# Weight sums of the seven-product blocks: formed by accumulating transfers in layer 0 instead of on VectorE

## The chip, the cores and the metric

The kernel runs on one core of a Trainium2 chip. The metric is the device time of one execution in microseconds (us). Engines are named as in the profile: PE is TensorE (matrix products), PEld its weight load, DVE is VectorE, ACT is ScalarE, POOL is GpSimd, SP is SyncE. Transfers are issued by an engine's instruction stream: SP issues most loads, POOL a second stream of loads and stores. Rows "SPq" and "POOLq" tell the two apart.

## The reference

Two layers of a diffusion backbone over 512 latent tokens and 256 context tokens, model width 1024. Each layer is modulation, attention, then a SwiGLU feed-forward. Only the feed-forward of layer 0 is changed in how its work is done:

```
def swiglu(h, w_gate_up, w_down):
    g, u = jnp.split(h @ w_gate_up, 2, axis=-1)
    return (jax.nn.silu(g) * u) @ w_down

h_lat = h_lat + g_f * swiglu(modulate(h_lat, sh_f, sc_f), ffn_w_gate_up[l], ffn_w_down[l])
if ctx_out:            # layer 0 only
    h_ctx = h_ctx + cg_f * swiglu(modulate(h_ctx, csh_f, csc_f), ffn_w_gate_up[l], ffn_w_down[l])
```

The hidden width is 2816, that is 22 blocks of 128 columns, called j below.

## The kernel before

**Products in three parts.** Every fp32 operand is split into a high part (an ACT cast, L1401 or L308) and a low part (operand minus high part, DVE, L1402 or L309). One product is high·high, high·low and low·high, so three matmuls for each slice of 128 in the contraction (L1414, L1415, L1416).

**Seven products in place of eight.** In a feed-forward block j≥2 of layer 0, gate weights g and up weights u (each 128 x 1024) form a 2 x 2 block matrix with two halves of the contraction, g1, g2, u1, u2, each 128 x 512. The tokens form the other 2 x 2 matrix. Class Pair computes the four result blocks with seven block products: `head` does 11 (with g1) and 21 (with g2); `body` does T2 (with the weight sum s2), T3 (s3) and T1 (s1); `tail` does 22 (s4) and T4 (u2). One block product is 12 matmuls of 128 x 384. `sums()` forms the token sums once for each layer.

**Weights of one pair.** `weights()` loads g and u, 512 KB each, through SP into `wr` tiles, and forms on DVE s1 = u1+u2 (L1436, tile pl), s2 = s1−g1 (L1437, ph), s3 = g1−u1 (L1440, ph) and s4 = g2−s2 (L1444, pl). Then `parts` splits g, s2, s3, s1, s4 and u2 for PE. T3 and T2 share the `wh`/`wl` tile of s3 and s2; T1 and 22 share that of s1 and s4.

**Staging.** `ffn()` walks over chunks of hidden blocks: in layer 0 (0–3), (4–7), (8–11), (12–15), (16–19), (20–21). Blocks 0 and 1 do all eight products directly, so 20 pairs remain in layer 0, and 19 in layer 1. After a chunk, `down0` runs for 8 output blocks m: load home[m] through POOL (L1255, 384 KB), multiply the chunk with w_dn (L319–L322), add on DVE (L1251), store home[m] through POOL (L1568). The w_dn loads go through SP into `wr` tiles too.

**Other work laid beside it.** `late_mods` prepares modulation for layer 1 during this stage: a 512 KB load through POOL into one of the `rope` tiles (L263), then reductions on DVE (L273) that wait for its landing. Each step of it is placed by `late_step` at a point of the pairs.

**What sets the order.** A scheduler that simulates a timeline puts the instructions of every engine in order, and each engine then runs its own in that order. Tiles rotate: wr, wh and wl have 3 buffers each, ph and pl 4 each, p 8. A load into a tile waits until the last readers of that buffer are done.

Of the kernel before, what the change touches and what calls it, by code (L numbers as in the profile page):

```python
# [12 lines left out]
ALU = mybir.AluOpType  # L13

P = 128
# [71 lines left out]
def pieces(c):  # L87

    cut = [(slice(max(c.start, x.start), min(c.stop, x.stop)), v) for v, x in enumerate((LATS, CTXS))]
    return [(x, v) for x, v in cut if x.start < x.stop]  # L90
# [8 lines left out]
def hybrid_kernel(ctx: ExitStack, tc, I, out):  # L99
# [6 lines left out]
    def T(tag, shape, dt=F32):  # L106
        count[0] += 1
        if tag not in SIZES:
            return sb.tile(shape, dt, tag=tag, name=f"{tag}_{count[0]}", bufs=BUFS.get(tag, 1))
        n = int(np.prod(shape[1:]))  # L110
        t = sb.tile([P, SIZES[tag] // (2 if dt == mybir.dt.bfloat16 else 4)], dt, tag=tag, name=f"{tag}_{count[0]}",
                    bufs=BUFS[tag])[: shape[0], :n]
        if len(shape) == 3:
            t = t.rearrange("p (a b) -> p a b", a=shape[1])
        return t

    def B(dt=F32, tag="b"):
        return T(tag, [P, NT], dt)
# [12 lines left out]
    V, S, G, PE = nc.vector, nc.scalar, nc.gpsimd, nc.tensor  # L131

    def dma(o, i, eng=None):
        return (eng or nc.sync).dma_start(f(o), f(i))

    def f(ap):
        return ap.bitcast(F32) if ap.dtype == F32R else ap

    silu, marks = [], {}

    def behind(ins, *before):

        for x in before:
            tc.add_manual_dep(ins.ins, x.ins.name, mybir.DependencyInfo(mybir.DependencyClass.NoSync,
                              mybir.DependencyReason.DATA), reason="products in one run")
        return ins
# [148 lines left out]
    def mod(*which):  # L295
        while which not in MOD:
            bg()
        return MOD[which]
# [593 lines left out]
    for c in range(4):  # L892
# [9 lines left out]
        s0, m0, s1, m1 = turns_of  # L902
# [424 lines left out]
    def combined(src, l, comp, c1, c2):  # L1327

        ops = {x: [] for x in ("11", "12", "21", "22", "T1", "T2", "T3", "T4")}
        far, near, spare, w = [], [], [], c1.stop  # L1330
        at1, at2, at3 = (slice(i * w, i * w + w) for i in range(3))
        narrow, room = 3 * w <= NT, {}

        def unit(tag):

            if not room.get(tag):
                t = B(F32R, tag)
                room[tag] = [t[:, i * w : i * w + w] for i in range(NT // w)]
            return room[tag].pop(0)

        def modulated_to(t, src, k, r, c, at, after=()):
            for x, v in pieces(c):
                d = t[:, at + x.start - c.start : at + x.stop - c.start]
                behind(V.scalar_tensor_tensor(d, src[:, x], mod(l, comp + 1, v, k), r[:, x], op0=ALU.mult, op1=ALU.mult), *after)
                S.activation(d, d, AF.Identity, bias=mod(l, comp, v, k), scale=1.0)

        def several(t, names, tag):

            dst, n = (B(F32R, tag), B(F32R, tag)), len(names) * w
            h, lo = split(t[:, :n], dst=dst)  # L1350
            near_done.append(marks["split"])
            near_cast.append(marks["cast"])
            for i, x in enumerate(names):
                ops[x].append((h[:, i * w : i * w + w], lo[:, i * w : i * w + w]))
            return h[:, n:], lo[:, n:]

        def use(k, r, c, v):
            i, half = k % 4, k // 4
            at = w * half
            if c is c2:  # L1360
                if half == 0:
                    far.append(B())
                modulated_to(far[i], src[k], k, r, c, at)
                name, tag = ("12", "22")[half], ("st", "b")[half]
                if narrow and half == 0:
                    t = T(("ph", "pl")[i % 2], [P, 2 * w], F32R)
                    h, lo = t[:, :w], t[:, w:]
                else:
                    h, lo = unit(tag), unit(tag)
                ops[name].append(parts(far[i][:, at : at + w], h, lo))  # L1370
                return
            if half == 0:
                near.append(B(tag="p"))
            modulated_to(near[i], src[k], k, r, c, at, near_done[-2:-1])
            if half == 1:
                spare.append(several(near[i], ("11", "21"), "b"))

        def sums():

            for i in range(4):  # L1380
                tag = "st" if i < 2 else "b"
                x, y = B(tag="p"), B(tag="p")
                b11, b21, b12, b22 = near[i][:, at1], near[i][:, at2], far[i][:, at1], far[i][:, at2]
                V.tensor_tensor(x[:, at1], b12, b11, op=ALU.subtract)
                V.tensor_tensor(x[:, at2], b22, x[:, at1], op=ALU.subtract)
                if narrow:
                    V.tensor_tensor(x[:, at3], b22, b12, op=ALU.subtract)
                    several(x, ("T1", "T2", "T3"), tag)
                    V.tensor_tensor(y[:, at1], b21, x[:, at2], op=ALU.subtract)
                    ops["T4"].append(parts(y[:, at1], *spare[i]))  # L1390
                    continue
                several(x, ("T1", "T2"), tag)
                V.tensor_tensor(y[:, at1], b22, b12, op=ALU.subtract)
                V.tensor_tensor(y[:, at2], b21, x[:, at2], op=ALU.subtract)
                several(y, ("T3", "T4"), tag)

        near_done.clear(), near_cast.clear()
        return Norm(src, use, G if l else None, (0, 4, 1, 5, 2, 6, 3, 7)), ops, sums

    def parts(t, h, lo, after=()):  # L1400
        S.copy(h, t)  # L1401
        marks["low"] = behind(V.tensor_tensor(lo, t, f(h), op=ALU.subtract), *after)  # L1402
        return h, lo
# [14 lines left out]
    class Pair:  # L1418
# [7 lines left out]
        def weights(self):  # L1426
            h = [slice(0, 512), slice(512, 1024)]
            g, u = T("wr", [P, D]), T("wr", [P, D])
            dma(g, I["w_gu"][self.l, self.j, 0])
            dma(u, I["w_gu"][self.l, self.j, 1])  # L1430
            two = lambda: (T("wh", [P, D], F32R), T("wl", [P, D], F32R))
            w1, w2, w3 = two(), two(), two()
            parts(g, *w1, self.after)
            self.g1, self.g2 = ([x[:, y] for x in w1] for y in h)
            s1, s2 = T("pl", [P, 512]), T("ph", [P, 512])
            behind(V.tensor_tensor(s1, u[:, h[0]], u[:, h[1]], op=ALU.add), *self.after)  # L1436
            V.tensor_tensor(s2, s1, g[:, h[0]], op=ALU.subtract)  # L1437
            self.s2 = parts(s2, *(x[:, h[0]] for x in w2))
            s3 = T("ph", [P, 512])
            behind(V.tensor_tensor(s3, g[:, h[0]], u[:, h[0]], op=ALU.subtract), *self.after)  # L1440
            self.s3 = parts(s3, *(x[:, h[1]] for x in w2))
            self.s1 = parts(s1, *(x[:, h[0]] for x in w3))
            s4 = T("pl", [P, 512])
            V.tensor_tensor(s4, g[:, h[1]], s2, op=ALU.subtract)  # L1444
            self.s4 = parts(s4, *(x[:, h[1]] for x in w3))
            self.u2 = parts(u[:, h[1]], T("ph", [P, 512], F32R), T("pl", [P, 512], F32R))

# [10 lines left out]
        def body(self):  # L1458
            self.y = PG()[:, : self.w]
            product(self.z, self.s2, self.ops["T2"])  # L1460
            S.copy(self.t[:, self.c1], self.z)
            product(self.y, self.s3, self.ops["T3"], True)
            product(self.z, self.s1, self.ops["T1"])
            S.copy(self.t[:, self.c2], self.z)  # L1464
            self.done = marks["middle"] = V.tensor_tensor(self.t[:, self.c2], self.y, self.t[:, self.c2], op=ALU.add)

        def tail(self):
            product(self.z, self.s4, self.ops["22"])
            marks["silu"] = S.activation(self.s[:, self.c2], self.z, AF.Silu)
            product(self.y, self.u2, self.ops["T4"])  # L1470
            V.tensor_tensor(self.t[:, self.c1], self.y, self.t[:, self.c1], op=ALU.add)
            for c in (self.c2, self.c1) if self.w > NX else (slice(0, 2 * self.w),):
                V.tensor_tensor(self.s[:, c], self.s[:, c], self.t[:, c], op=ALU.mult)
                parts(self.s[:, c], *(x[:, c] for x in self.dst))
            self.done = marks["low"]
# [369 lines left out]
```

## Time and profile before

| what | value |
|---|---|
| median of 3 runs | 1554.84 us (1552.52 to 1556.6) |
| span of the profiled execution | 1553.0 us |
| PE busy | 1527.4 us, 98% of the span |
| DVE busy | 1179.9 us, 76% |
| ACT busy | 758.2 us, 49% |
| POOL busy | 195.1 us, 13% |
| feed-forward of layer 0 | about 455 to 955 us of the span |
| DMA queue of SP (q1) | 148.47 MB, 30.1% of 16 engines' span |
| DMA queue of POOL (q0) | 73.94 MB, 13.9% |

The profiled execution was not timed in another way than by its span, which lies 1.8 us below the median of the runs and within their spread. PE is nearly always busy, so what counts is the few places where PE stands still. The share of DVE says nothing by itself of the time.

### The profile page before, as it was taken

Reading aid. Unit: us, or ns where it says so; the run is one execution under the profiler, and the core shown is the slowest. Engines: PE = TensorE matmul, PEld = TensorE weight load, DVE = VectorE, ACT = ScalarE, POOL = GpSimd, SP = SyncE. Lnnn points to the kernel's source line nnn. Section 1 sums busy time; section 2 is a strip of 40 time slices with the busy share of each in tenths; the row PEclk is TensorE's granted clock in tenths of the full one; section 3 lists DMA queues with packets and bytes.
Section 4 is the critical chain, followed back from the end, with each engine's and each line's share of the span. In section 5 each row is a group of like instructions: output and inputs, shape, how many; then the busy total and the mean of one; then the engine's idle time right before and its main releaser. Section 6 shows DMA issues by size and latency. Waiting matters only on the chain.

```text
span 1553.0 us, 26645 instructions
## 1 busy us (share of the span) xinstructions
PE 1527.4 (98%) x10048; PEld 1375.5 (89%) x10048; DVE 1179.9 (76%) x2418; ACT 758.2 (49%) x1521; POOL 195.1 (13%) x266
## 2 busy tenths in 40 slices
PE   9999999999999999999999999999999999999997
PEld 8788887878999898999989998877789899899997
DVE  4799877776867686777768667789977779678685
ACT  4532676674555242432424335567856445354453
POOL 0022211000111102012021122560011000000001
PEclk9999999999999999999999999999999999999999
DMA  9775654244643636547475493210214223324322
GB/s 320 251 226 176 165 129 106 57 131 136 217 138 119 232 104 216 173 133 287 128 261 175 156 355 137 59 37 1 96 58 161 70 84 127 115 75 136 89 91 87
DMA packets 80930, 225.69 MB, mean 145 GB/s; under 512 B 11232, under 2 KB 18400, under 8 KB 80800
## 3 DMA queue, kind: packets, MB, share of 16 engines
q1 hardware_dynamic: 61968, 148.47, 30.1%
q0 software_dynamic: 17680, 73.94, 13.9%
q8 instruction: 79, 1.29, 0.3%
q10 hardware_dynamic: 1152, 1.57, 0.3%
q14 instruction: 51, 0.42, 0.1%
HBM read 186.97 MB, written 23.07 MB: 135 GB/s over the span
## 4 chain that ended last, share of the span: by engine, by line
PE 85%; DVE 7%; DMA 3%; ACT 2%; issue 2%; POOL 0%; SPq 0%; DVEq 0%; ACTq 0%; POOLq 0%
PE pso L530 5%; PE pss L1416 5%; PE pss L1415 5%; PE pss L1414 5%; PE psd L319 4%; PE pss L319 4%; PE psd L321 4%; PE psd L322 4%; PE pss L322 4%; PE pss L321 4%; PE pst L1416 3%; PE pst L319 3%; PE pst L321 3%; PE pst L1414 3%; PE pst L322 3%; PE pst L1415 3%
## 5 line engine op out<-in xcount | busy, mean ns | idle before, releaser
L308 ACT CAST wh<-wr 128x1024 fp32r<-128x1024 f32 (+2 forms) x148 | 115.6, 795 | 225.1 <-DMA wr<-in_w_dn_dram 39.4
L309 DVE TENSOR_TENSOR wl<-wr,wh 128x1024 fp32r<-128x1024 f32 (+2 forms) x145 | 131.1, 911 | 82.3 <-ACT wh L308 78.1
L537 ACT ACTIVATE p<-p,sm 128x512 f32<-128x512 f32 (+3 forms) x144 | 105.0, 730 | 30.6 <-DVE sm L541 30.1
L1414 PE MATMUL pss<-b,wh 128*128 128x384 f32 (+1 forms) x346 | 107.6, 312 | 0.5 <-ACT b L345 0.5
L1415 PE MATMUL pss<-b,wh 128*128 128x384 f32 (+1 forms) x346 | 107.8, 312 | 0.0
L1416 PE MATMUL pss<-b,wl 128*128 128x384 f32 (+1 forms) x346 | 107.1, 311 | 0.0
L321 PE MATMUL psd<-b,wh 128*128 128x512 f32 (+2 forms) x254 | 88.7, 349 | 0.0
L273 DVE CUSTOM_DVE_ANT_0 p<-rope,cond 128x1024 bf16<-128x1024 f32 x64 | 76.9, 1221 | 12.4 <-DMA rope<-in_mod_w_dram 12.1
L319 PE MATMUL psd<-b,wh 128*128 128x512 f32 (+2 forms) x214 | 79.0, 369 | 0.7 <-ACT wh L308 0.3
L322 PE MATMUL psd<-b,wl 128*128 128x512 f32 (+2 forms) x214 | 77.8, 363 | 0.0
L263 POOL DMA_DIRECT2D rope<-in_mod_w_dram x48 | 25.6, 533 | 412.4 <-DVE mod L273 389.8
L530 PE MATMUL pso<-ph,b 128*64 128x256 f32 (+1 forms) x384 | 77.0, 359 | 0.2 <-DVE ph L475 0.2
L530 PE MATMUL pso<-pl,b 128*64 128x256 f32 (+1 forms) x384 | 76.9, 358 | 0.0
L1416 PE MATMUL pst<-b,wl 128*128 128x384 f32 (+1 forms) x226 | 70.8, 313 | 2.0 <-DVE wl L1402 2.0
L1414 PE MATMUL pst<-b,wh 128*128 128x384 f32 (+1 forms) x226 | 70.7, 313 | 0.6 <-ACT p L1464 0.6
L1401 ACT CAST wh<-pl 128x512 fp32r<-128x512 f32 x78 | 44.9, 619 | 53.0 <-PE pss L1415 22.7
L1415 PE MATMUL pst<-b,wh 128*128 128x384 f32 (+1 forms) x226 | 70.5, 312 | 0.0
L1401 ACT CAST wh<-wr 128x1024 fp32r<-128x1024 f32 x39 | 41.0, 1051 | 57.3 <-PE pst L1415 14.8
L321 PE MATMUL pss<-b,wh 128*128 128x256 f32 (+3 forms) x216 | 68.3, 316 | 0.0
L319 PE MATMUL pss<-st,wh 128*128 128x512 f32 (+2 forms) x198 | 67.5, 341 | 0.3 <-ACT wh L308 0.3
L322 PE MATMUL pss<-st,wl 128*128 128x512 f32 (+2 forms) x198 | 67.6, 341 | 0.1
L1414 PEld LDWEIGHTS pss<-b,wh 128*128 128x128 f32 x346 | 65.0, 188 | 1.0 <-ACT b L345 0.8
(609 smaller groups left out, 5269.4 us busy)
## 6 DMA issues: line engine op xcount, KB each, us to landing
wr<-in_w_gu_dram SPq DMA_DIRECT2D x88, 512.0 KB, 4.0
rope<-in_mod_w_dram POOLq DMA_DIRECT2D x48, 512.0 KB, 3.9
wr<-in_w_dn_dram SPq DMA_DIRECT2D x73, 256.0 KB, 3.0
wr<-in_w_out_dram SPq DMA_DIRECT2D x32, 512.0 KB, 3.8
p<-home POOLq DMA_DIRECT2D x40, 384.0 KB, 5.7
home<-p POOLq DMA_DIRECT2D x40, 384.0 KB, 5.6
wr<-in_w_in_dram SPq DMA_DIRECT2D x21, 512.0 KB, 3.9
ph<-in_mod_w_dram SPq DMA_DIRECT2D x24, 256.0 KB, 3.0
```

The source lines that it names most:

```text
L273: behind(V.tensor_tensor_reduce(out=T("p", [P, D], mybir.dt.bfloat16), in0=w, in1=cond[:, v, :], op0=ALU.mult, op1=ALU.add, scale=1.0, sca ...
L308: behind(S.copy(h, r), *after[:1])
L309: behind((G if eng else V).tensor_tensor(lo, r, f(h), op=ALU.subtract), *after[1:])
L319: ins = PE.matmul(o, wh[:, k], mh[:, c], start=first and k == 0, stop=False)
L321: PE.matmul(o, wh[:, k], ml[:, c], start=False, stop=False)
L322: PE.matmul(o, wl[:, k], mh[:, c], start=False, stop=last and k == n - 1)
L530: ins = PE.matmul(o[64 * i : 64 * i + 64, c], v(kt), t, start=n == 0, stop=n == len(moving[i]) - 1)
L537: S.activation(p[:, c], p[:, c], AF.Exp, bias=nm, scale=-1.0, accum_out=dn)
L1401: S.copy(h, t)
L1414: PE.matmul(o, wh, xh, start=first and k == 0, stop=False, skip_group_check=not first)
L1415: PE.matmul(o, wh, xl, start=False, stop=False, skip_group_check=not first)
L1416: PE.matmul(o, wl, xh, start=False, stop=k == 3, skip_group_check=not first)
```

## The change

All signs of the seven-product scheme are turned so that s1 to s4 are additions: the token sums in `sums()`, and the additions of results in `body` and `tail`, take the opposite signs. In layer 0 each weight sum is then made without DVE. A plain load through SP (256 KB) brings one operand into the tile, and an accumulating transfer through POOL adds the other: s1 takes u2 from DRAM, s2 takes s1 from SBUF, s3 takes u1 from DRAM, s4 takes s2 from SBUF. Of u only the second half is loaded into `wr`. Layer 1 keeps four DVE additions for each pair.

```
         def weights(self):
             h = [slice(0, 512), slice(512, 1024)]
             g, u = T("wr", [P, D]), T("wr", [P, D])
-            dma(g, I["w_gu"][self.l, self.j, 0])
-            dma(u, I["w_gu"][self.l, self.j, 1])
+            dg, du = I["w_gu"][self.l, self.j, 0], I["w_gu"][self.l, self.j, 1]
+            by_dma = self.l == 0
+            dma(g, dg)
+            if by_dma:
+                dma(u[:, h[1]], du[:, h[1]])
+            else:
+                dma(u, du)
...
+            def total(tag, a, b, da, db, after=()):
+                s = T(tag, [P, 512])
+                if by_dma:
+                    dma(s, da)
+                    G.dma_start(s, db if db is not None else b, accum_op=ALU.add)
+                else:
+                    behind(V.tensor_tensor(s, a, b, op=ALU.add), *after)
+                return s
+
             parts(g, *w1, self.after)
...
-            behind(V.tensor_tensor(s1, u[:, h[0]], u[:, h[1]], op=ALU.add), *self.after)
-            V.tensor_tensor(s2, s1, g[:, h[0]], op=ALU.subtract)
+            s1 = total("pl", u[:, h[0]], u[:, h[1]], du[:, h[0]], du[:, h[1]], self.after)
+            s2 = total("ph", g[:, h[0]], s1, dg[:, h[0]], None)
...
-            behind(V.tensor_tensor(s3, g[:, h[0]], u[:, h[0]], op=ALU.subtract), *self.after)
+            s3 = total("ph", g[:, h[0]], u[:, h[0]], dg[:, h[0]], du[:, h[0]], self.after)
...
-            V.tensor_tensor(s4, g[:, h[1]], s2, op=ALU.subtract)
+            s4 = total("pl", g[:, h[1]], s2, dg[:, h[1]], None)
...
         sums():
-                V.tensor_tensor(x[:, at1], b12, b11, op=ALU.subtract)
-                V.tensor_tensor(x[:, at2], b22, x[:, at1], op=ALU.subtract)
+                V.tensor_tensor(x[:, at1], b11, b12, op=ALU.subtract)
+                V.scalar_tensor_tensor(x[:, at2], b22, -1.0, x[:, at1], op0=ALU.mult, op1=ALU.subtract)
...
         body():
-            self.done = marks["middle"] = V.tensor_tensor(self.t[:, self.c2], self.y, self.t[:, self.c2], op=ALU.add)
+            self.done = marks["middle"] = V.tensor_tensor(self.t[:, self.c2], self.y, self.t[:, self.c2], op=ALU.subtract)
```

Two places of the order are needed later. The first is POOL's stream for the last pairs of chunk 8–11. In before it stands as follows: `rope` tiles are late modulation weights, `home` the residual rows.

```order
L263 DMA rope_1518_7223<-in_mod_w_dram 128x1024
L263 DMA rope_1521_7267<-in_mod_w_dram 128x1024
L263 DMA rope_1543_7368<-in_mod_w_dram 128x1024
L1255 DMA p_7452<-home_4265 128x768
L263 DMA rope_1546_7412<-in_mod_w_dram 128x1024
```

In the changed kernel the same stretch of POOL's stream holds the sums of pair 11 (s1 in pl_7319, s2 in ph_7322, s4 in pl_7334; s3, in ph_7327, stands just ahead) and those of pair 12, which belongs to the next chunk (s3 in ph_7821, s1 in pl_7813, s2 in ph_7816, s4 in pl_7828):

```order
L263 DMA rope_1491_7105<-in_mod_w_dram 128x1024
L1443 DMA pl_7319<-in_w_gu_dram 128x512
L1443 DMA ph_7322<-pl_7319 128x512
L263 DMA rope_1495_7153<-in_mod_w_dram 128x1024
L1443 DMA pl_7334<-ph_7322 128x512
L263 DMA rope_1518_7259<-in_mod_w_dram 128x1024
L1443 DMA ph_7821<-in_w_gu_dram 128x512
L1443 DMA pl_7813<-in_w_gu_dram 128x512
L263 DMA rope_1521_7303<-in_mod_w_dram 128x1024
L1443 DMA ph_7816<-pl_7813 128x512
L1443 DMA pl_7828<-ph_7816 128x512
L263 DMA rope_1543_7408<-in_mod_w_dram 128x1024
```

So the accumulates of pairs 11 and 12 now stand between the modulation loads, all four of pair 12 ahead of rope_1543. SP's stream holds the plain loads for the same tiles, between the w_dn loads (`wr` from in_w_dn):

```order
L134 DMA wr_7454<-in_w_dn_dram 128x512
L134 DMA ph_7322<-in_w_gu_dram 128x512
L134 DMA ph_7327<-in_w_gu_dram 128x512
L134 DMA pl_7319<-in_w_gu_dram 128x512
L134 DMA pl_7334<-in_w_gu_dram 128x512
L134 DMA wr_7531<-in_w_dn_dram 128x512
L134 DMA wr_7568<-in_w_dn_dram 128x512
L134 DMA ph_7816<-in_w_gu_dram 128x512
L134 DMA ph_7821<-in_w_gu_dram 128x512
L134 DMA pl_7813<-in_w_gu_dram 128x512
L134 DMA pl_7828<-in_w_gu_dram 128x512
L134 DMA wr_7609<-in_w_dn_dram 128x512
```

Before, w_dn loads followed one another on SP here, and the loads of the next chunk's first pair stood behind the last of them. Now the four loads of pair 12 stand among the w_dn loads. The ph and pl tiles have 4 buffers each and one pair takes three of each, so such a load waits until a sum of the pair before has been read: ph_7327 (s3 of pair 11) waits for the landing of the accumulate of s4 of pair 10, since that is the last reader of the buffer, and pl_7319 (s1 of pair 11) stands behind it.

The second place is DVE's stream at the end of chunk 8–11. In before (wl_7531 is the low part of the third w_dn block, p_7303 and b_7123 the hidden results):

```order
L273 ISA p_7366,mod_1516_7220<-rope_1521_7267,cond_70 128x1024
L273 ISA mod_1516_7220 128x1
L309 TENSOR_TENSOR wl_7494<-wr_7491,wh_7493 128x512
L1465 TENSOR_TENSOR p_7304<-pss_7370,p_7304 128x384
L273 ISA p_7410,mod_1516_7220<-rope_1543_7368,cond_70 128x1024
L273 ISA mod_1516_7220 128x1
L309 TENSOR_TENSOR wl_7531<-wr_7528,wh_7530 128x512
```

And in the changed kernel:

```order
L273 ISA p_7406,mod_1516_7256<-rope_1521_7303,cond_70 128x1024
L273 ISA mod_1516_7256 128x1
L309 TENSOR_TENSOR wl_7534<-wr_7531,wh_7533 128x512
L1477 TENSOR_TENSOR p_7344<-pss_7410,p_7344 128x384
L273 ISA p_7450,mod_1516_7256<-rope_1543_7408,cond_70 128x1024
L273 ISA mod_1516_7256 128x1
L309 TENSOR_TENSOR wl_7571<-wr_7568,wh_7570 128x512
```

Nothing moved here: the reduction that waits for rope_1543 stands ahead of the low part of the third w_dn block in both. What moved is the load it waits for, which now stands behind the accumulates of pair 12. On PE the order of the block products in a chunk of four pairs: products of a pair are interleaved with those of the next, the first two matmuls of T3 of a pair stand right behind its products 11 and 21, and for pair 11 these are behind the 20th product of the chunk. The slot into which s1's parts of pair 9 go comes free with the 6th product (21 of pair 9), and the third w_dn block's first use stands behind 28 products and 36 matmuls of the first two w_dn blocks.

More of the change, by code (lines that the diff above doesn't have):

```diff
@@ L1383, in sums @@
                 b11, b21, b12, b22 = near[i][:, at1], near[i][:, at2], far[i][:, at1], far[i][:, at2]
-                V.tensor_tensor(x[:, at1], b12, b11, op=ALU.subtract)
-                V.tensor_tensor(x[:, at2], b22, x[:, at1], op=ALU.subtract)
+                V.tensor_tensor(x[:, at1], b11, b12, op=ALU.subtract)
+                V.scalar_tensor_tensor(x[:, at2], b22, -1.0, x[:, at1], op0=ALU.mult, op1=ALU.subtract)
                 if narrow:
-                    V.tensor_tensor(x[:, at3], b22, b12, op=ALU.subtract)
+                    V.tensor_tensor(x[:, at3], b12, b22, op=ALU.subtract)
                     several(x, ("T1", "T2", "T3"), tag)
-                    V.tensor_tensor(y[:, at1], b21, x[:, at2], op=ALU.subtract)
+                    V.tensor_tensor(y[:, at1], b21, x[:, at2], op=ALU.add)
                     ops["T4"].append(parts(y[:, at1], *spare[i]))
@@ L1392, in sums @@
                 several(x, ("T1", "T2"), tag)
-                V.tensor_tensor(y[:, at1], b22, b12, op=ALU.subtract)
-                V.tensor_tensor(y[:, at2], b21, x[:, at2], op=ALU.subtract)
+                V.tensor_tensor(y[:, at1], b12, b22, op=ALU.subtract)
+                V.tensor_tensor(y[:, at2], b21, x[:, at2], op=ALU.add)
                 several(y, ("T3", "T4"), tag)
@@ L1428, in weights @@
             g, u = T("wr", [P, D]), T("wr", [P, D])
-            dma(g, I["w_gu"][self.l, self.j, 0])
-            dma(u, I["w_gu"][self.l, self.j, 1])
+            dg, du = I["w_gu"][self.l, self.j, 0], I["w_gu"][self.l, self.j, 1]
[5 more added lines that the diff above has]
+                dma(u, du)
             two = lambda: (T("wh", [P, D], F32R), T("wl", [P, D], F32R))
             w1, w2, w3 = two(), two(), two()
+            def total(tag, a, b, da, db, after=()):
[6 more added lines that the diff above has]
+                return s
             parts(g, *w1, self.after)
             self.g1, self.g2 = ([x[:, y] for x in w1] for y in h)
-            s1, s2 = T("pl", [P, 512]), T("ph", [P, 512])
-            behind(V.tensor_tensor(s1, u[:, h[0]], u[:, h[1]], op=ALU.add), *self.after)
-            V.tensor_tensor(s2, s1, g[:, h[0]], op=ALU.subtract)
+            s1 = total("pl", u[:, h[0]], u[:, h[1]], du[:, h[0]], du[:, h[1]], self.after)
+            s2 = total("ph", g[:, h[0]], s1, dg[:, h[0]], None)
             self.s2 = parts(s2, *(x[:, h[0]] for x in w2))
-            s3 = T("ph", [P, 512])
-            behind(V.tensor_tensor(s3, g[:, h[0]], u[:, h[0]], op=ALU.subtract), *self.after)
+            s3 = total("ph", g[:, h[0]], u[:, h[0]], dg[:, h[0]], du[:, h[0]], self.after)
             self.s3 = parts(s3, *(x[:, h[1]] for x in w2))
             self.s1 = parts(s1, *(x[:, h[0]] for x in w3))
-            s4 = T("pl", [P, 512])
-            V.tensor_tensor(s4, g[:, h[1]], s2, op=ALU.subtract)
+            s4 = total("pl", g[:, h[1]], s2, dg[:, h[1]], None)
             self.s4 = parts(s4, *(x[:, h[1]] for x in w3))
@@ L1470, in tail @@
             product(self.y, self.u2, self.ops["T4"])
-            V.tensor_tensor(self.t[:, self.c1], self.y, self.t[:, self.c1], op=ALU.add)
+            V.tensor_tensor(self.t[:, self.c1], self.y, self.t[:, self.c1], op=ALU.subtract)
             for c in (self.c2, self.c1) if self.w > NX else (slice(0, 2 * self.w),):
```

## The prediction

> **What bounds the kernel now.** I read the engine table and the chain of the page first, then a table of the stage that the change touches, then what PE waits for in it.
>
> ```profile
> span 1553.0 us, 26645 instructions
> PE 1527.4 (98%) x10048; PEld 1375.5 (89%) x10048; DVE 1179.9 (76%) x2418; ACT 758.2 (49%) x1521; POOL 195.1 (13%) x266
> PE 85%; DVE 7%; DMA 3%; ACT 2%; issue 2%; POOL 0%; SPq 0%; DVEq 0%; ACTq 0%; POOLq 0%
> ```
>
> PE is busy 98% of the span; DVE, which the change relieves, is second and holds 7% of the chain. The next view cuts layer 0's feed-forward into stretches, roughly one for each chunk (PE is the first pair of columns, the last three are PE's granted clock, the DMA share and GB/s).
>
> ```profile
> 455.00:531.00 76.00, 75.48 (x460) 68.77 (x459) 50.60 (x92) 28.92 (x51) 12.58 (x24) 1.00 0.43 149
> 531.00:623.00 92.00, 91.22 (x520) 86.43 (x519) 70.50 (x122) 31.46 (x59) 12.00 (x23) 1.00 0.54 184
> 623.00:715.00 92.00, 90.65 (x518) 86.29 (x517) 67.89 (x118) 33.21 (x61) 11.23 (x21) 1.00 0.49 165
> 715.00:807.00 92.00, 92.00 (x528) 87.78 (x527) 68.67 (x118) 32.41 (x60) 14.99 (x28) 1.00 0.60 205
> 807.00:899.00 92.00, 92.00 (x528) 87.80 (x527) 68.33 (x118) 32.63 (x60) 14.99 (x28) 1.00 0.57 205
> 899.00:955.00 56.00, 54.74 (x302) 50.56 (x301) 40.67 (x65) 24.15 (x40) 12.54 (x20) 1.00 0.70 254
> sum 500.00, PE 496.10 PEld 467.63 DVE 366.67 ACT 182.78 POOL 78.33; mean PE 82.68 PEld 77.94 DVE 61.11 ACT 30.46 POOL 13.05
> ```
>
> PE is idle 500.00 − 496.10 = 3.9 us in the whole stage, and not at all in two of the stretches. That is the ceiling of what less work on DVE can bring here: 3.9 us are 0.25% of the time, under the 0.3% (4.7 us) that a measurement of this kernel can tell from no change. The clock is 1.00 everywhere, so no stretch is held by it. A full stretch runs 528 matmuls in 92.00 us, 0.174 us each; I use that step below. What ends PE's idle time:
>
> ```profile
> PE pst L1416 <- DVE wl L1402: 2.0, 2, 1.4
> PE psd L319 <- DVE p L1251: 0.7, 1, 0.7
> PE pst L1414 <- ACT p L1464: 0.6, 1, 0.6
> PE pss L1414 <- ACT b L345: 0.5, 1, 0.5
> ```
>
> Two waits of 2.0 us in all are for DVE's low parts of the weight sums. The chain ahead of the longer one shows what stood there:
>
> ```profile
> 630.74 5.82 DMA wr<-in_w_gu_dram
> ...
> 638.48 0.60 DVE ph L1437
> ...
> 639.60 0.68 DVE pl L1444
> ...
> 641.36 1.14 DVE wl L1402
> 642.50 0.04 issue
> 642.54 0.44 PE pst L1416
> ```
>
> So a crowded weight load (5.82 us) came late, and the sums behind it (L1437, L1444) were part of the delay.
>
> **What is removed.** In the same stage DVE has these groups (busy us, mean ns; then idle before):
>
> ```profile
> L273 DVE CUSTOM_DVE_ANT_0 p<-rope,cond 128x1024 bf16<-128x1024 f32 x56 | 67.5, 1221 | 12.1 <-DMA rope<-in_mod_w_dram 11.9
> L309 DVE TENSOR_TENSOR wl<-wr,wh 128x512 fp32r<-128x512 f32 (+1 forms) x44 | 32.1, 737 | 42.7 <-ACT wh L308 42.7
> L1402 DVE TENSOR_TENSOR wl<-pl,wh 128x512 fp32r<-128x512 f32 x40 | 26.2, 688 | 13.1 <-ACT wh L1401 13.0
> L1436 DVE TENSOR_TENSOR pl<-wr 128x512 f32<-128x512 f32 x19 | 13.1, 687 | 12.0 <-DMA wr<-in_w_gu_dram 12.0
> L1444 DVE TENSOR_TENSOR pl<-wr,ph 128x512 f32<-128x512 f32 x19 | 13.0, 685 | 0.0
> ```
>
> 20 pairs times four sums of 0.69 us are 55 us of DVE's 1179.9. DVE is off the path but for the few waits above, so I credit 3 us of PE's 3.9, not 55: the remainder (ACT, L1251) has nothing to do with the sums. The turned signs cost nothing: additions and subtractions have the same rows, and the one new form (L1385, a scalar_tensor_tensor in place of a subtract) runs 8 times; were each to cost a whole sum's 0.69 us more, that is 5.5 us on DVE beside PE's work.
>
> **What is added.** For each layer-0 pair, four 256 KB loads on SP, against one half of u (256 KB) saved, and four accumulates of 256 KB on POOL. First two rows of the stage for the steps used below (an ACT cast, POOL's time to issue), then the page's transfers (KB each, us from issue to landing):
>
> ```profile
> L1401 ACT CAST wh<-pl 128x512 fp32r<-128x512 f32 x40 | 23.0, 619 | 40.1 <-PE pss L1415 18.7 <-PE pst L321 12.6 <-PE pst L1415 7.7
> L263 POOL DMA_DIRECT2D rope<-in_mod_w_dram x44 | 23.4, 532 | 262.1 <-DVE mod L273 239.5 <-DVE wl L1402 8.8 <-PE pst L212 7.6
> ```
>
> ```profile
> wr<-in_w_gu_dram SPq DMA_DIRECT2D x88, 512.0 KB, 4.0
> ...
> wr<-in_w_dn_dram SPq DMA_DIRECT2D x73, 256.0 KB, 3.0
> ```
>
> And the same in the stage's middle alone (470 to 900 us), with its queues (packets, MB, share of 16 engines):
>
> ```profile
> q0 software_dynamic: 12085, 51.23, 34.1%
> q1 hardware_dynamic: 10368, 27.53, 18.9%
> ...
> rope<-in_mod_w_dram POOLq DMA_DIRECT2D x43, 512.0 KB, 3.9
> wr<-in_w_gu_dram SPq DMA_DIRECT2D x35, 512.0 KB, 5.5
> p<-home POOLq DMA_DIRECT2D x37, 384.0 KB, 5.7
> ...
> wr<-in_w_dn_dram SPq DMA_DIRECT2D x39, 256.0 KB, 3.7
> nb<-in_mod_wp_dram POOLq DMA_DIRECT2D x2, 256.0 KB, 3.0
> rope<-in_mod_wp_dram POOLq DMA_DIRECT2D x2, 256.0 KB, 4.3
> ```
>
> POOL's issues cost nothing by themselves: 80 more at 0.53 us are 43 us on an engine with 78.33 of 500 us busy. The engines of the DMA are another matter. By the queue rows 1 MB takes 0.341·430/51.23 = 2.9 us of all 16 on either queue. A pair adds 0.75 MB on SP and 1 MB on POOL (2 MB if the destination's reading counts): 5 to 8 us. About 18 pairs lie in these 430 us, so the share goes from 53% to between 74 and 86%. There is room, but transfers will meet more often.
>
> No row of before shows an accumulate. Call its time from issue to landing A. Bounds: 3.0 us (256 KB on POOL's queue alone, nb) and 5.7 us (home rows, the slowest kind). I take 4.3, the row of 256 KB that are issued on the same queue directly behind another transfer, since every accumulate stands so.
>
> [...]
>
> **Where A lies on a path.** The four sums of a pair are a chain: s1, then s2 which reads s1, then s4 which reads s2, each waiting for the landing of the last. And pairs are chained too, since ph and pl have four buffers: a pair's s1 load stands on SP behind s3's, whose buffer comes free when s4 of the pair before has landed. In a chunk of four pairs (8 to 11, time from its first matmul): the slot for s1's parts of pair 9 is free after 6 products of 12 matmuls, 72·0.174 = 12.5, cast 0.62, low part 0.69: 13.8. A 256 KB load takes 3.0 on the page and 3.7 here; I take 3.35. Then s1 of pair 10 is loaded at 17.2, and s4 of pair 10 lands at 17.7 + 3A with one rope issue (0.53) between. Pair 11's s1 load: 21.0 + 3A; behind two issues (s3's accumulate and a rope load) its accumulate lands at 22.1 + 4A, s2's at 22.1 + 5A, and two casts make it 23.3 + 5A. PE needs T3 of pair 11, which ACT casts behind s2, right after 20 products: 240·0.174 = 41.8. So PE is late by 5A − 18.5, that is 3.0 us at 4.3; the threshold is A = 3.7.
>
> The second place is the chunk's end. s4 of pair 11 lands at 22.6 + 6A; s1 of pair 12 is loaded at 26.0 + 6A, its s1 and s2 accumulates with a rope issue between end at 26.5 + 8A, and only then do s4's accumulate and rope_1543 issue (1.06). The rope lands 3.9 later, its reduction takes 1.22 and the low part of the third w_dn block, queued behind it on DVE, 0.74: 33.4 + 8A. Waiting behind that reduction are also the hidden results of pair 11. PE wants that block after 372 matmuls, 64.7. So PE is late by 8A − 31.3, 3.1 us at 4.3; the threshold is 3.9. Both are the same delay seen twice, not two: the larger counts, 3.1 to 3.2. Four chunks of four pairs end so: 4·3.2 = 13 us. In the chunks with two pairs the chain is too short to be late.
>
> **The sum.** −3 + 13 = +10 us. Against the profiled span, 1553.0 becomes 1563; the runs' median lies 1.8 us higher, so 1565.
>
> **Rivals.**
> - *The accumulate is as quick as a plain transfer, A at most 3.9.* Then the lateness is 5·3.9 − 18.5 = 1.0 us for a chunk or nothing, and +4 − 3 to −3.9: 1551 to 1557, no change that can be told. For it: rope's 512 KB in 3.9 and nb's 3.0. Against: the DMA share goes up by 20 to 33 points, and w_gu's 4.0 on the page is 5.5 in this stage already. [...]
> - *The accumulate is slow, A from 5 up.* At 5.7 the chunk's end is late by 8·5.7 − 31.3 = 14.3, four times 57: 1609; at 5 it is 8.7, 35 − 3: 1587. For it: 5.7 for home rows on the same queue, and three transfers in the chain must each wait for the one ahead. Against: home rows are larger and meet each other.
> - *Faster: sums off DVE close every gap.* The windows of 531 to 715 us hold 520 and 518 matmuls against 528, 18·0.174 = 3.1 us lost where their idle columns say 2.1; on the whole 3.9 that scales to 5.8 us: 1549. It decides only with A under 3.7, and if the two waits on ACT and L1251 go too, which the sums did not cause.
>
> **How the numbers follow.** Forecast (A about 4 to 4.9): 0.40, 1558 to 1584. No change: 0.31. Slow accumulate: 0.22. Faster: 0.07. So slower by over 0.3% has 0.40 + 0.22 = 0.62, within 0.3% 0.31, faster 0.07. The range runs from 1551 (all of PE's idle time gone) to 1598 (A = 5.3: 11.1·4 − 3 = +41, and 1.8 more for scatter); what is left out is most of the faster case and the slow end, near 0.15.
>
> **What would show it.** In the profile after, the accumulates are rows of POOL's transfers with their time to landing: A itself. If I am right it is 4 to 5 us; PE waits for ACT's casts of s3 at T3 of the chunk's last pair and for DVE's low part of w_dn at the chunk's end, about 3 us each time; DVE's wait for rope grows past 11.9 us; DVE's busy time falls by about 55 us with no gain from it; the DMA share in the chunks rises to 70–85%. Wrong, if PE stays at 92.00 of 92 in all four chunks (no change), or if PE's waits lie elsewhere: at the heads of pairs, when w_gu loads are late on SP behind loads that wait for a buffer.

## The result and the profile after

The changed kernel takes 1624.83 us (1623.24 to 1631.24, 4 runs), against 1555.72 us for the kernel before on the same chip: a ratio of 1.0459, interval 1.0441 to 1.0477. It is 69 us slower. The page after, with the same lines as shown of before:

```profile
span 1623.1 us, 26904 instructions
PE 1553.3 (96%) x10048; PEld 1387.4 (85%) x10048; DVE 1134.8 (70%) x2338; ACT 757.9 (47%) x1521; POOL 267.0 (16%) x346
```

DVE is relieved by 45 us (1179.9 to 1134.8), and the span of the profiled execution is 70 us longer (1553.0 to 1623.1). PE's idle time goes from 25.6 to 69.8 us, and its busy time, with the same 10048 matmuls, from 1527.4 to 1553.3. These are the stretches of layer 0's feed-forward, which now runs to about 1027 us (same columns as before):

```profile
531.00:640.00 109.00, 95.92 (x528) 89.80 (x527) 63.82 (x109) 32.05 (x59) 26.50 (x39) 0.97 0.76 218
640.00:740.00 100.00, 87.10 (x472) 81.61 (x471) 50.76 (x87) 30.95 (x57) 22.27 (x31) 0.97 0.74 206
740.00:840.00 100.00, 90.77 (x492) 83.06 (x492) 55.25 (x93) 30.27 (x56) 27.81 (x41) 0.98 0.83 245
840.00:940.00 100.00, 94.85 (x517) 87.30 (x515) 57.70 (x98) 32.53 (x60) 27.32 (x41) 0.98 0.86 257
940.00:1025.00 85.00, 79.68 (x424) 70.97 (x425) 50.97 (x83) 28.80 (x49) 23.45 (x37) 0.98 0.76 260
```

The loss is in every stretch, and the granted clock, 1.00 in all of them before, is 0.97 to 0.98. How long one chunk lasts can be read from the timeline, at the first matmul of chunk 8–11 and of chunk 12–15:

```profile
654.96 0.34 PE L1414 MATMUL pss<-b,wh 128*128 128x384 f32 x1
...
765.04 0.34 PE L1414 MATMUL pss<-b,wh 128*128 128x384 f32 x1
```

That is 110.1 us. In the kernel before the same two matmuls stood 94.0 us apart:

```profile
631.98 0.34 PE L1414 MATMUL pss<-b,wh 128*128 128x384 f32 x1
...
726.01 0.34 PE L1414 MATMUL pss<-b,wh 128*128 128x384 f32 x1
```

Measured so, the four chunks of four pairs grew by 16.1, 16.0, 14.2 and 13.4 us, 60 of the 70; 6 more came ahead of the first product of pair 2 (470.36 to 476.41; why was not followed), and the first chunk and the last (20, 21) added 4.4. What PE waits for in the stage:

```profile
PE pss L322 <- DVE wl L309: 11.7, 5, 3.0
PE pss L1416 <- DVE wl L1402: 8.0, 2, 4.9
PE psd L1414 <- ACT wh L1401: 6.8, 3, 3.9
PE pss L1414 <- ACT wh L1401: 4.7, 3, 2.4
PE psd L1414 <- DVE p L1251: 3.9, 3, 1.3
```

Low parts of w_dn (L309, 11.7 us) and casts of sums (L1401, 6.8 + 4.7 = 11.5 us) lead. These are the two kinds of wait that the prediction named. The 8.0 us for low parts of weights inside a chunk (L1402) it did not name. DVE itself waits for the modulation loads, for 11.9 us before and now for 63.0:

```profile
DVE p L273 <- DMA rope<-in_mod_w_dram: 63.0, 21, 7.8
```

And the transfers of the stage's middle (470 to 950 us), from issue to landing:

```profile
rope<-in_mod_w_dram POOLq DMA_DIRECT2D x41, 512.0 KB, 5.6
...
ph<-in_w_gu_dram POOLq DMA_DIRECT2D x18, 256.0 KB, 4.7
pl<-ph POOLq DMA_DIRECT2D x18, 256.0 KB, 3.9
pl<-in_w_gu_dram POOLq DMA_DIRECT2D x17, 256.0 KB, 6.4
ph<-pl POOLq DMA_DIRECT2D x17, 256.0 KB, 3.4
```

The last four rows are the accumulates of s3, s4, s1 and s2. The median of all is 4.7 us, close to the 4.3 assumed; but s1's takes 6.4. In 14 of these 17 pairs another transfer goes out on POOL's queue at most 1.2 us ahead of it: s3's accumulate, a modulation load or a row of `home`. For s2's and s4's accumulates the transfer ahead is 5.25 and 3.67 us off (medians). The modulation loads on the same queue rose from 3.9 to 5.6.

### The profile page after: what moved, and what is told of

It reads as the page before. It is cut to its first block, busy times and chain, and to the rows that moved or that the text cites. A ratio compares the mean times of both kernels' runs of the same rounds, so it can differ in the third digit from the quotient of the medians.

```text
span 1623.1 us, 26904 instructions
## 1 busy us (share of the span) xinstructions
PE 1553.3 (96%) x10048; PEld 1387.4 (85%) x10048; DVE 1134.8 (70%) x2338; ACT 757.9 (47%) x1521; POOL 267.0 (16%) x346
## 5 line engine op out<-in xcount | busy, mean ns | idle before, releaser
L309 DVE TENSOR_TENSOR wl<-wr,wh 128x1024 fp32r<-128x1024 f32 (+2 forms) x145 | 130.8, 910 | 71.4 <-ACT wh L308 67.1
L1414 PE MATMUL pss<-b,wh 128*128 128x384 f32 (+1 forms) x346 | 109.9, 318 | 6.3 <-ACT wh L1401 4.1
L1415 PE MATMUL pss<-b,wh 128*128 128x384 f32 (+1 forms) x346 | 109.1, 315 | 0.0
L1402 DVE TENSOR_TENSOR wl<-ph,wh 128x512 fp32r<-128x512 f32 x78 | 51.4, 686 | 51.1 <-ACT wh L1401 50.9
L1401 ACT CAST wh<-ph 128x512 fp32r<-128x512 f32 x78 | 45.9, 620 | 79.7 <-DMA ph<-pl 29.6
L322 PE MATMUL pss<-st,wl 128*128 128x512 f32 (+2 forms) x198 | 69.2, 350 | 11.8 <-DVE wl L309 11.7
L1416 PEld LDWEIGHTS pss<-b,wl 128*128 128x128 f32 x346 | 66.2, 192 | 9.6 <-DVE wl L1402 9.6
L1401 ACT CAST wh<-pl 128x512 fp32r<-128x512 f32 x78 | 45.9, 619 | 59.1 <-DMA pl<-ph 27.1
```

Of the source, the lines that this page charges most:

```text
L309: behind((G if eng else V).tensor_tensor(lo, r, f(h), op=ALU.subtract), *after[1:])
L322: PE.matmul(o, wl[:, k], mh[:, c], start=False, stop=last and k == n - 1)
L1414: PE.matmul(o, wh, xh, start=first and k == 0, stop=False, skip_group_check=not first)
L1415: PE.matmul(o, wh, xl, start=False, stop=False, skip_group_check=not first)
L1416: PE.matmul(o, wl, xh, start=False, stop=k == 3, skip_group_check=not first)
```

## The round of one pair

POOL's timeline in chunk 8–11 (start, duration of the issue, and in brackets POOL's idle time and what ended it) shows the serial round. `pl<-in_w_gu` is s1, `ph<-pl` s2, `pl<-ph` s4, `ph<-in_w_gu` s3:

```profile
669.05 0.87 POOL L1443 DMA_DIRECT2D pl<-ph  x1 [6.99 <-DMA ph<-pl]
675.69 0.87 POOL L1443 DMA_DIRECT2D ph<-in_w_gu_dram  x1 [5.77 <-DMA ph<-in_w_gu_dram]
676.47 0.99 POOL L1443 DMA_DIRECT2D pl<-in_w_gu_dram  x1
677.01 1.01 POOL L263 DMA_DIRECT2D rope<-in_mod_w_dram  x1
683.62 0.87 POOL L1443 DMA_DIRECT2D ph<-pl  x1 [5.60 <-issue]
687.41 0.87 POOL L1443 DMA_DIRECT2D pl<-ph  x1 [2.92 <-DMA ph<-pl]
694.25 0.88 POOL L1443 DMA_DIRECT2D ph<-in_w_gu_dram  x1 [5.97 <-DMA ph<-in_w_gu_dram]
694.80 0.89 POOL L263 DMA_DIRECT2D rope<-in_mod_w_dram  x1
695.88 0.87 POOL L1443 DMA_DIRECT2D pl<-in_w_gu_dram  x1 [0.19 <-issue]
702.40 0.87 POOL L1443 DMA_DIRECT2D ph<-pl  x1 [5.65 <-DMA pl<-in_w_gu_dram]
```

s4 of pair 9 is issued at 669.05. It lands, s3 of pair 10 is loaded through SP into the buffer that it frees, and only at 675.69 can s3's accumulate go; s1's follows at once. POOL then stands until s2's accumulate, which reads s1, is issued at 683.62 (in the next round, at 702.40, the row names s1's landing as what ended the wait). s4 of pair 10 follows at 687.41, when s2 has landed. From s4 to s4 are 18.4 us; the next two rounds end at 706.26 and 727.56, 18.9 and 21.3 us. PE needs 7 products, 84 matmuls of 0.174 us, 14.6 us for a pair. Each of these rounds is slower than PE.

The same rows show a second mechanism. The modulation load at 694.80 stands in POOL's order behind s3's accumulate, before which POOL stood for 5.97 us until s3's plain load had landed. DVE waits for that modulation load until 700.84, and the low part of g, which stands behind the reductions in DVE's order, comes so late that PE waits too (DVE's rows, then PE's):

```profile
700.84 1.23 DVE L273 CUSTOM_DVE_ANT_0 p<-rope,cond 128x1024 bf16<-128x1024 f32 x1 [7.38 <-DMA rope<-in_mod_w_dram]
...
703.13 1.22 DVE L1402 TENSOR_TENSOR wl<-wr,wh 128x1024 fp32r<-128x1024 f32 x1
```

```profile
704.41 0.45 PE L1416 MATMUL pss<-b,wl 128*128 128x384 f32 x1 [3.14 <-DVE wl L1402]
```

## Experiments

In each run below the scheduler put the instructions in order anew, so small differences of order come with every edit. Times of before on the same chips were 1554.5 to 1555.5 us.

**The signs alone.**

```
-            by_dma = self.l == 0
+            by_dma = False
```

> The turned signs alone; all four sums stay on VectorE in both layers, no accumulating transfers. Every theory expects no change: 1551 to 1560 us, PE idle about 4 us in layer 0's feed-forward. If it is 10 us or more slower, the signs or the order that came with them have a part in the 69 us.

1555.47 us, ratio 1.0007 (0.9998 to 1.0017). The signs and the order that comes with them cost nothing.

**Loads without accumulates.**

```
                 if by_dma:
                     dma(s, da)
-                    G.dma_start(s, db if db is not None else b, accum_op=ALU.add)
```

> The accumulates are left out and the plain loads of the first operands stay (so each sum is its first operand only): SyncE's traffic and order as in the changed kernel, nothing added on GpSimd. Two-mechanism theory: 1552 to 1560, nothing left of the loss. Traffic theory: 0.75 MB of the 1.75 to 2.75 MB added for a pair stay, 1570 to 1580.

Each sum is then its first operand alone. 1557.57 us, ratio 1.0009 (0.9993 to 1.0024). Two things follow. SP's 80 loads, the halved u and their order cost nothing. And DVE is relieved just as in the changed kernel,

```profile
PE 1525.5 (98%) x10048; PEld 1373.4 (88%) x10048; DVE 1134.8 (73%) x2338; ACT 758.6 (49%) x1521; POOL 195.0 (13%) x266
```

with no time gained: the four DVE additions of a pair were hidden. So the loss, all of it within the interval, comes with the accumulates. This run does not say by which way: their wait for one another, their place in POOL's order, or their traffic.

**Plain transfers in place of accumulates.**

```
-                    G.dma_start(s, db if db is not None else b, accum_op=ALU.add)
+                    G.dma_start(s, db if db is not None else b)
```

> The 80 accumulating transfers become plain transfers of the same operand, on the same queue with the same waits (the addition is left out, so the sums hold only their second operand). Chain theory (s1, s2, s4 and the buffer of the next pair wait for one another, about 18 us for a pair where PE needs 14.6): a plain 256 KB that is second on the queue took 4.3 us before against 6.4 now, so the round falls to about 15 us and most of the loss goes, 1565 to 1575. Traffic theory (the DMA engines at 74 to 86% make every transfer late): only the destination's reading goes, 1 of 2.75 MB added for a pair, about 1595 to 1605.

The additions are left out, and each sum holds its second operand. 1584.56 us, ratio 1.0194 (1.0172 to 1.0216): 30 of 69 us are left, between the two forecasts, so this run alone does not decide. s1's transfer fell from 6.4 to 4.5 us (rows of s3, s4, s1, s2):

```profile
ph<-in_w_gu_dram POOLq DMA_DIRECT2D x18, 256.0 KB, 3.8
pl<-ph POOLq DMA_DIRECT2D x18, 256.0 KB, 3.5
pl<-in_w_gu_dram POOLq DMA_DIRECT2D x17, 256.0 KB, 4.5
ph<-pl POOLq DMA_DIRECT2D x17, 256.0 KB, 3.2
```

So with the accumulation s1's transfer, which has company on the queue, took 1.9 us longer, s3's 0.9, and those of s2 and s4, which mostly go alone, 0.2 and 0.4.

**Accumulates that wait for no other.**

```
-            s2 = total("ph", g[:, h[0]], s1, dg[:, h[0]], None)
+            s2 = total("ph", g[:, h[0]], s1, dg[:, h[0]], du[:, h[1]])
-            s4 = total("pl", g[:, h[1]], s2, dg[:, h[1]], None)
+            s4 = total("pl", g[:, h[1]], s2, dg[:, h[1]], du[:, h[0]])
```

> s2 and s4 accumulate a weight operand from DRAM in place of s1 and s2 (so those two sums are other sums than the reference needs): the same number and size of accumulates and loads, but none waits for the landing of another. Chain theory: the loss goes, 1555 to 1570. Traffic theory: the traffic is the same, so 1610 to 1630. Queue theory (modulation loads and residual rows stuck on GpSimd's in-order queue behind accumulates that wait): in between, since accumulates still wait for their loads and buffers, 1580 to 1600.

s2 and s4 are then other sums than the products need. 1603.85 us, ratio 1.0327 (1.0304 to 1.0351): 49 us are left. The chain theory in its plain form fell; the queue theory's 1580 to 1600 and the traffic theory's 1610 to 1630 both missed too. What took its place stands in the trace. PE has one wait of 4.2 us around 682 us, for DVE's low parts, and POOL and DVE at that time show why:

```profile
675.02 1.14 POOL L1443 DMA_DIRECT2D ph<-in_w_gu_dram  x1
676.06 0.65 POOL L263 DMA_DIRECT2D rope<-in_mod_w_dram  x1
```

```profile
683.33 1.23 DVE L273 CUSTOM_DVE_ANT_0 p<-rope,cond 128x1024 bf16<-128x1024 f32 x1 [5.89 <-DMA rope<-in_mod_w_dram]
...
685.62 1.22 DVE L1402 TENSOR_TENSOR wl<-wr,wh 128x1024 fp32r<-128x1024 f32 x1
```

This modulation load, issued at 676.06 directly behind an accumulate, lets its reduction begin only 7.3 us later; DVE stands idle for 5.89 us before the reduction, and the low part of g, which PE needs, is behind it in DVE's order. It is the second mechanism of the changed kernel's own rows above. In that run DVE waits 64.5 us for these loads, no less than with the chain.

**Modulation loads through SyncE.** In `fetch_unit`:

```
-            G.dma_start(w, I["mod_w"][l * 48 + comp * 8 + m])
+            dma(w, I["mod_w"][l * 48 + comp * 8 + m])
```

> The changed kernel with the late modulation loads issued by SyncE in place of GpSimd, so that they neither wait behind accumulates nor go ahead of them. Queue theory: most of the loss goes, 1570 to 1585. Chain theory: each rope load stood ahead of one accumulate of the chain for 2 us or so, and the low parts behind the reductions are no longer held, yet the round of the three accumulates stays longer than PE's: 1600 to 1615. Traffic theory: no change, 1620 to 1630.

1611.84 us, ratio 1.0382 (1.0363 to 1.0401): 57 us are left, in the range of the chain theory. DVE's wait for the modulation loads is nearly halved (63.0 to 34.2 us). PE now waits for ACT, for its copies of results (L1476) and for casts of sums (L1401):

```profile
PE pst L1414 <- ACT p L1476: 12.0, 6, 4.3
PE psd L1414 <- ACT wh L1401: 11.7, 6, 3.5
```

**Both.** The two edits above together.

> Both at once: s2 and s4 accumulate from DRAM (other sums than the reference needs), so no accumulate waits for another, and the late modulation loads go through SyncE. Two-mechanism theory (the serial chain of accumulates, and modulation loads that arrive late behind accumulates on GpSimd's queue while VectorE's in-order stream holds low parts behind them): each change alone left 49 and 57 of the 69 us since the other mechanism took over; both together take most away, 1560 to 1575. Traffic theory (the DMA engines are too full, whatever the queue): as with the chain off alone, 1595 to 1605.

1569.45 us, ratio 1.0077 (1.0046 to 1.0108). This is in the range of the two mechanisms (1560 to 1575). Alone the edits won 21 and 13 us, together 55: each mechanism had taken over where the other was removed. This run also speaks against the traffic theory, which had 1595 to 1605. The stage's middle (470 to 930 us) without the chain, and then with both edits:

```profile
470.00:930.00 460.00, 428.96 (x2363) 399.82 (x2362) 268.23 (x461) 148.34 (x272) 122.86 (x182) 0.97 0.80 232
```

```profile
470.00:930.00 460.00, 452.96 (x2573) 422.69 (x2573) 295.54 (x504) 160.48 (x290) 112.12 (x160) 1.00 0.87 258
```

The DMA engines are busier (0.87 against 0.80, the last column but one), at the same transfers for each pair, and PE is nearly full with its clock at 1.00 (the column before). Not the amount of traffic was the trouble, but which transfers stood behind which on one queue, and who waited for them.

**A control for the moved loads.** The kernel before, with the `fetch_unit` edit only.

> The kernel before with only the late modulation loads moved to SyncE; a control for what the move itself gives without any accumulate. Every theory: 1551 to 1560, within 0.3% of before, since PE is idle for only 3.9 us in this stage. If it gains 5 us or more, part of what the moved loads gave in the other runs is not owed to the accumulates.

1564.02 us, ratio 1.0046 (1.0026 to 1.0065). The expectation missed: by the ratio the move costs 7 us by itself. In SP's order other loads now stand behind modulation loads, and those wait for DVE's reductions (us in total, times, longest):

```profile
SPq L134 <- DVE mod L273: 130.4, 43, 11.6
```

That these waits are the whole of the 7 us was not shown.

**Both, with plain transfers.** The run with both edits, and `accum_op=ALU.add` taken out.

> As the run with both changes (accumulates from DRAM that wait for no other, modulation loads on SyncE), with plain transfers in place of the accumulates (the additions are left out). If the 14 us still lost there are owed to the accumulates' longer landing (6.4 us in the crowd): 1553 to 1560. If they are owed to the number of transfers and waits in the order: 1565 to 1572.

1561.64 us, ratio 1.0034 (1.0020 to 1.0049), between the two forecasts. By the ratios 12 us were left with both edits and 5 are left here, about the 7 of the control. So, as an estimate, 5 to 7 us are the moved loads and about as much is what accumulation adds to a transfer's issue and landing; the interval of the run with both edits alone is 5 us either way.

**Half of the sums.** s1 and s3 by accumulating transfers, s2 and s4 on DVE:

```
-            s2 = total("ph", g[:, h[0]], s1, dg[:, h[0]], None)
+            s2 = T("ph", [P, 512])
+            V.tensor_tensor(s2, g[:, h[0]], s1, op=ALU.add)
...
-            s4 = total("pl", g[:, h[1]], s2, dg[:, h[1]], None)
+            s4 = T("pl", [P, 512])
+            V.tensor_tensor(s4, g[:, h[1]], s2, op=ALU.add)
```

> Only s1 and s3 are formed by accumulating transfers (both from DRAM), s2 and s4 by additions on VectorE, as the reference needs. Two-mechanism theory: no chain of accumulates, half as many ahead of the modulation loads, so 1558 to 1570. Traffic theory: half of the loss, 1585 to 1595. A version that beats the kernel before would be under 1550.

1583.19 us, ratio 1.0176 (1.0143 to 1.0209), above the forecast of 1558 to 1570 and below the rival's 1585 to 1595. And the same with the modulation loads on SP:

> s1 and s3 by accumulating transfers, s2 and s4 on VectorE, and the late modulation loads on SyncE: a correct kernel with neither a chain of accumulates nor modulation loads behind them. Two-mechanism theory: 1555 to 1563, so most of the 28 us that the half change still lost goes. If the rest of that loss is traffic: 1570 to 1583.

1577.31 us, ratio 1.0136 (1.0109 to 1.0164). This missed the forecast too and lies in the range written for traffic, 1570 to 1583. Yet the run with both edits has twice as many accumulates, the same moved loads, and takes 8 us less (1569.45), so the amount of traffic does not explain it; about 7 us are the moved loads, by the control. Its chunks 8–11 and 12–15, taken as above, last 94.8 and 94.4 us (before 94.0 and 92.4), so in the middle the loss is nearly gone. What is left stands at both ends, in chunk 4–7 and in the last, above all in waits for casts:

```profile
PE pss L1414 <- ACT wh L1401: 11.3, 3, 6.5
```

Why these came so late was not settled. No version tried is faster than the kernel before.

**One more buffer each.**

```
-BUFS = dict(b=24, part=4, st=12, wr=3, wh=3, wl=3, p=8, ph=4, pl=4, sm=10, nb=2)
+BUFS = dict(b=24, part=4, st=12, wr=3, wh=3, wl=3, p=7, ph=5, pl=5, sm=10, nb=2)
```

> The changed kernel with 5 buffers in place of 4 for ph and for pl (the room comes from p, 7 in place of 8): a pair's first loads no longer wait for s4 of the pair before. Two-mechanism theory: pairs overlap, so the part of the chain that runs over pairs goes, while the modulation loads stay late as in the run without the chain: 1595 to 1610. If the recurrence over the buffers has no part, 1620 to 1630; a p buffer less could cost some us of its own.

1615.99 us, ratio 1.0391 (1.0356 to 1.0426): 9 us better than the changed kernel, between the two forecasts. What a `p` buffer less costs is in this number and was not measured apart. DVE's wait for modulation loads is 72.6 us there: again the other mechanism took over.

## Why the prediction was wrong

**Right.** Slower; that DVE's relief brings almost nothing (the run without accumulates, where not even the 3 us credited show); two kinds of wait, T3's casts and the low part of w_dn; the typical landing A (4.7 us against 4.3); the DMA share of 74 to 86% (0.74 to 0.86 in the stretches). No change and faster are out. DVE's busy time fell by 45 us and not by 55, in part because its neighbouring rows overlap by about 0.1 us (the reduction at 700.84 lasts 1.23 us, the next row starts at 701.99), and the busy time counts an overlap once.

**The term that failed is the lateness of a chunk**, 3.2 us in the sum, where the four chunks grew by 13.4 to 16.1. Followed through chunk 8–11, whose first matmul is at 654.96:

- *Where the chain starts.* I let pair 10's s1 be loaded at 17.2, from the slot of pair 9's parts, and took pair 9's s4 as landed. SP's order has s3's load of pair 10 ahead, and that waits for s4 of pair 9, issued at 669.05, 14.1 us into the chunk. So s1's accumulate of pair 10 went out at 676.47, 21.5 into the chunk: 4.3 us later than assumed. PE's first wait for a cast came at T3 of pair 10, a pair earlier than I had it: 3.9 us until 688.16, behind the landing of pair 10's s2.
- *A is not one number.* s1's accumulate, with company on the queue, took 6.4 us here, s2's and s4's 3.4 and 3.9. s2's accumulate of pair 11 was issued at 702.40, 47.4 into the chunk, where the prediction had 22.1 + 4·4.3 = 39.3. A is in the round once for each of s1, s2 and s4 (6.4 + 3.4 + 3.9 = 13.7 us), and with the load and the issues the round is 18 to 21 us against PE's 14.6. Put into the formula of the chunk's end, these landings give 33.4 + 2·13.7 + 6.4 + 3.4 − 64.7 = 5.9 us; with the start 4.3 us later and a modulation load of 5.6 in place of 3.9 it is 11.9, an estimate. The rest of this chunk's 16.1 falls to the next point and to the clock; the two were not told apart.
- *"The same delay seen twice".* I took the larger of the two places. The runs show two mechanisms that both bind. I priced the modulation load at 3.9 us from before and let it be late only at the chunk's end. On the queue with the accumulates it took 5.6, it was issued late where an accumulate ahead of it waited (the one at 694.80, behind POOL's 5.97 us), and DVE waited for such a load 21 times in the stage (9 times before), not once for each chunk: 63 us of waiting, some of it ahead of parts that PE needed. PE's 8.0 us for L1402 are two such places, the one shown above and one at 591 us. Removing the chain alone left that.

The rival of slow accumulates had a price (1609) nearer the result, but for another reason than it gave: it needed A of 5.7.

**What I left out: the clock.** I read 1.00 in every stretch before and did not ask whether it would stay there once PE stands idle longer. Three windows of 10 us after:

```profile
585.00:595.00 10.00, 5.15 (x21) 0.76 0.70 177
...
685.00:695.00 10.00, 6.84 (x30) 0.83 0.61 147
695.00:705.00 10.00, 6.86 (x39) 1.00 0.64 139
```

(Columns: window, length, PE busy, clock, DMA share, GB/s.) After some of its waits PE ran at a lower granted clock for some us: from 689.5 to 692.5 it is 0.50, behind the wait of 3.9 us in the second row, and from 914 to 919 it is 0.66, behind one of 1.7 us that ended at 913.80. The 3.1 us wait in the third row is followed by a clock of 1.00 (704.5 to 709). So the length of a single wait does not decide here; what decides it was not shown. Over all windows of 10 us but the last ones, where the program ends, (1 − clock)·10 us sums to 18.7 us after and 3.4 before. That puts at most 15 of the 70 us to the clock, an estimate, since PE may also stand still in such a time; what it did cost is part of the 26 us by which PE's busy time grew.

## What to carry to other kernels

Before work is moved off an engine, look for the wait that it would shorten: here 45 us came off DVE and the time did not move (ratio 1.0009 in the run without accumulates), since PE was idle for only 3.9 us in that stage. When work is moved onto a queue, list what already stands in that queue and who waits for it in order; here modulation loads, behind which DVE held low parts, came later behind accumulates that had to wait, and DVE's waits for them went from 11.9 to 63.0 us. Serial transfers are priced by the round, landing plus load plus issue against the time that the bottleneck needs for one step (here 18 to 21 us against 14.6), and if the round is longer the loss comes at each step, not once.

## What the hardware showed that was not expected

An accumulating transfer took POOL longer to issue: 0.87 to 0.94 us in the means of the four sums (s2's and s3's below), against 0.54 for s3's as a plain one of the same size (the run with plain transfers, second block).

```profile
L1443 POOL DMA_DIRECT2D ph<-pl x19 | 17.8, 937 | 67.0 <-DMA pl<-in_w_gu_dram 49.2 <-issue 17.8
L1443 POOL DMA_DIRECT2D ph<-in_w_gu_dram x19 | 16.8, 886 | 75.9 <-DMA ph<-in_w_gu_dram 42.7 <-DVE p L1477 7.9 <-DVE pl L1402 6.1
```

```profile
L1443 POOL DMA_DIRECT2D ph<-in_w_gu_dram x19 | 10.2, 538 | 76.2 <-DMA ph<-in_w_gu_dram 37.7 <-DVE p L1477 11.5 <-DVE st L346 5.3
```

And an accumulate of 256 KB with other transfers close ahead of it on the queue (s1's) landed in 6.4 us, against 4.5 with plain transfers in the same places, where those that mostly go alone differ by 0.4 us at most (s2's 3.4 against 3.2, s4's 3.9 against 3.5).
